# The expert stage of a two-layer trunk: norm weights ahead of the gather, token weights at the read-out, pairs summed in PSUM

## The chip, the cores and the metric

One core of a Trainium2 chip runs the whole program. The metric is the device time of one execution in microseconds; less is better. All weights are read from HBM once. The engines named below are TensorE (matmuls), VectorE, ScalarE, GpSimd and SyncE, whose queue issues the weight transfers.

## The reference, cut

A trunk of two layers runs over 256 positions of width 1024. Each layer mixes (`w_in`, three kinds of heads, `w_out`), then has a feed-forward part (dense in layer 0, eight experts in layer 1, of which each token takes its best two), then a gated embedding. The change touches only the expert part of layer 1:

```python
def _moe_swiglu(x, router_w, wg, wu, wd):      # x: RMSNorm(h) * ffn_norm_g
    logits = (xt @ router_w).astype(jnp.float32)
    top_val, top_idx = lax.top_k(logits, TOP_K)
    gates = jax.nn.softmax(top_val, axis=-1)
    combine = jnp.einsum('nk,nke->ne', gates, jax.nn.one_hot(top_idx, N_EXPERTS))
    for e in range(N_EXPERTS):
        out = out + combine[:, e:e + 1] * _swiglu(xt, wg[e], wu[e], wd[e])
```

`_swiglu` is `(silu(x @ wg) * (x @ wu)) @ wd` with a hidden width of 3584.

## The kernel before

Matrix products use float32 numbers split into a rounded high half and a low half (type F32R), which TensorE takes in a single pass: hi x hi, hi x lo and lo x hi are summed in PSUM (`mm3`). Weights come in tiles of 128 x 2048 (1 MB). ScalarE makes `hi`, VectorE makes `lo` (`Feed.high`, `Feed.low`); nine tiles of raw weights (five `rawp`, four `rawb`) are in flight, and SyncE's queue loads the next when VectorE has done with one (`Feed.pump`, line 326).

The order of instructions is planned when the program is built. The main stream emits the matmuls; side streams (generators) emit everything else. `best` picks the side step with the least estimated start, and of equal ones the one with the smaller `pen`; `slot` lets steps in between two products; each engine then works its list in order.

The expert stage (`moe`) begins with the router: `choose` makes logits and the best two of each token, `ranks` counts tokens for each expert, sorts the experts by count (`order`, which the transfers of expert weights need) and gives each token a rank within its expert. `busy` adds a filler matmul of 512 columns of float32 that nothing reads. `normed` writes the normed tokens, without the norm's weights, as halves `ah` (named rh) and `al` (rl).

The eight experts are taken in four pairs (`FE`, `MOE`). Those with the most tokens (three, one in each of the first three pairs) have 128 slots, the others 64 (`SLOTS`). For a pair, `gather` makes one-hot matrices `P` from the ranks and `part` multiplies `ah` and `al` with them (32 matmuls of 256 columns into pgx), then `splits` multiplies by the norm's weights and splits again: 16 ScalarE and 16 VectorE instructions write `gx`. `turned` transposes P for the way back (`PT`).

Each expert has seven hidden blocks of 512. `gate_up` makes the two products (pmg, pmu), `gate` and `up` apply silu and multiply (msl) and split the result into `mt`; an expert with 64 slots keeps its two halves in one tile and folds them by eight small matmuls (msg, pht). `down` multiplies `mt` with the third matrix into pmy. After the seventh block `read_out` copies pmy (as two halves for 128 slots, whole for 64), `scatter` multiplies with PT into psc, and VectorE adds psc, times the token's weight `cp`, to `h`: eight additions for each pair.

The rank-sorted slots hold only 128 or 64 tokens. If an expert has more, `overflow` computes the rest in a general way: it is written out for all eight experts and two blocks, and stands behind a branch on the largest excess (line 1378, at the first products of expert 2). With the inputs given it is skipped.

In line 101 a helper issues all compute instructions, so views by line name it for nearly all of them; the names of the tiles tell them apart.

Of the kernel before, what the change touches and what calls it, by code (L numbers as in the profile page):

```python
# [22 lines left out]
NE = 8  # L23
# [41 lines left out]
def tile_trunk(ctx, tc, x, par, con, abias, wif, rw, pt, w1, w2, wgu, wdn, wpg, wpp, wm, out):  # L65
# [197 lines left out]
    nc.gpsimd.memset(ones, 1.0)  # L263
    euler = cst.tile([128, 1], F32, name="euler")
# [785 lines left out]
    def moe(L, X, nxt):  # L1050
# [11 lines left out]
        al = big.tile([128, 2, D], F32R, name="rl", tag="xh")  # L1062

        def normed(t):

            for f in range(2):
                s = slice(512 * f, 512 * f + 512)
                yield when(act, (X, t, "r"))
                act.activation(ah[:, t, s], h[:, t, s], AF.Copy, scale=X.of(t))
                yield when(dve, *[("ranks", 1) if f else ("order",)] * t)  # L1070
                dve.scalar_tensor_tensor(al[:, t, s], h[:, t, s], X.of(t), ah[:, t, s].bitcast(F32),
                                         op0=ALU.mult, op1=ALU.subtract)
                set_ready(("normed", t, f))

        def choose(t):
# [7 lines left out]
            busy(t)  # L1083
# [27 lines left out]
        def busy(t):  # L1111

            p = bank([128, 512], "busy")
            c, cur[0] = cur[0], None
            pe.matmul(p, lhsT=ident, rhs=h[:, t, 0:512], start=True, stop=True)
            cur[0] = c
            rel(p)

        def ranks():

            pr = bank([128, 3, NE], "prk")
            for t in range(2):
# [6 lines left out]
                busy(t)  # L1129
# [45 lines left out]
        Xe, PT, HT, SL, Y, YS = {}, {}, {}, {}, {}, {}  # L1175

        def gather(j2):

            P = F["P"].tile([128, 2, 2, 128], F32R, name="P", tag="P", bufs=1)
            for t in range(2):  # L1180
                yield when(dve, ("ranks", t))
                for j in range(2):
                    e = 2 * j2 + j
                    dve.tensor_scalar(P[:, t, j], iota if SLOTS[e] == 128 else twice, rp[:, t, e:e + 1], None,
                                      op0=ALU.is_equal)
            for j in range(2):
                e = 2 * j2 + j
                Xe[e] = big.tile([128, KT, 2, SLOTS[e]], F32R, name="gx", tag=("al", "xl")[j])
# [3 lines left out]
        def part(j2, P, k2):  # L1192
            ks = (2 * k2, 2 * k2 + 1)
            yield when(pe, ("normed", 0, k2 // 2), ("normed", 1, k2 // 2))
            p = bank([128, 4, 128], "pgx")
            for i2, k in enumerate(ks):
                for t in range(2):
                    for i, a in enumerate((ah, al)):
                        pe.matmul(p[:, 2 * i2:2 * i2 + 2].rearrange("p a b -> p (a b)"),
                                  lhsT=a[:, t, 128 * k:128 * k + 128],  # L1200
                                  rhs=P[:, t].rearrange("p a b -> p (a b)"), start=t + i == 0, stop=t + i == 2)
            xs = [(Xe[2 * j2 + j][:, k], p[:, 2 * i2 + j, :SLOTS[2 * j2 + j]], g[:, k:k + 1])
                  for j in range(2) for i2, k in enumerate(ks)]
            yield from splits(*[(v[:, 0], v[:, 1], src, gk) for v, src, gk in xs])
            rel(p)
            set_ready(("X", j2, k2))

        def turned(e, P):
            yield when(pe, ("X", e // 2, KT // 2 - 1))
# [65 lines left out]
        def overflow():  # L1275

            def part(src):
                r = F["P"].tile([128, 512], F32, name="or", tag="myh")
# [3 lines left out]
            r2 = F["P"].tile([128, 2, NE], F32, name="r2", tag="r2", bufs=1)  # L1282
            dve.tensor_tensor(r2, rm, slots[:, None, :].to_broadcast([128, 2, NE]), op=ALU.subtract)
            for e, block in [(e, b) for b in range(2) for e in range(NE)]:
                if not e:
                    dve.tensor_scalar(r2, r2, -(64.0, 128.0)[block], None, op0=ALU.add)
                P = F["P"].tile([128, 2, 2, 128], F32R, name="oP", tag="P", bufs=1)[:, :, 0]
                p = bank([128, 2, 128], "opt")
                for t in range(2):
                    dve.tensor_scalar(P[:, t], iota, r2[:, t, e:e + 1], None, op0=ALU.is_equal)  # L1290
                    pe.transpose(p[:, t], P[:, t].bitcast(F32), ident)
                T = F["P"].tile([128, 2, 128], F32, name="oT", tag="myl")
                act.activation(T, p, AF.Copy)
                rel(p)
                xf = F["T"].tile([128, KT, 128], F32, name="oxf", tag="mt")
                y = F["T"].tile([128, 2, 512], F32, name="oy", tag="mt")
                dve.memset(y, 0.0)
                for k in range(KT):
                    s = slice(128 * k, 128 * k + 128)
                    p = bank([128, 128], "ogx")  # L1300
                    for t in range(2):
                        pe.matmul(p, lhsT=ah[:, t, s], rhs=P[:, t], start=t == 0, stop=False)
# [372 lines left out]
```

## Time and profile before

| | us |
|---|---|
| median of 3 runs | 1451.82 (1448.79 to 1453.56) |
| profiled execution | 1451.61 |
| its span in the profile | 1449.9 |
| TensorE busy in the span | 1378.6 (95%) |
| VectorE busy | 1217.4 (84%) |
| ScalarE busy | 1048.0 (72%) |

The trace lists every instruction with its start and duration and, in brackets, the idle time of its engine before it and what ended that. Matmuls are pipelined: their durations overlap, and the distance between two starts is the price of one. A float32 matmul is two records, a single-pass one is one record.

### The profile page before, as it was taken

Reading aid. Unit: us, or ns where it says so; the run is one execution under the profiler, and the core shown is the slowest. Engines: PE = TensorE matmul, PEld = TensorE weight load, DVE = VectorE, ACT = ScalarE, POOL = GpSimd, SP = SyncE. Lnnn points to the kernel's source line nnn. Section 1 sums busy time; section 2 is a strip of 40 time slices with the busy share of each in tenths; the row PEclk is TensorE's granted clock in tenths of the full one; section 3 lists DMA queues with packets and bytes.
Section 4 is the critical chain, followed back from the end, with each engine's and each line's share of the span. In section 5 each row is a group of like instructions: output and inputs, shape, how many; then the busy total and the mean of one; then the engine's idle time right before and its main releaser. Section 6 shows DMA issues by size and latency. Waiting matters only on the chain. (4 is left out here: it accounts for less than half of the span.)

```text
span 1449.9 us, 18234 instructions
## 1 busy us (share of the span) xinstructions
PE 1378.6 (95%) x6426; PEld 1114.1 (77%) x6426; DVE 1217.4 (84%) x1294; ACT 1048.0 (72%) x1221; POOL 57.0 (4%) x71
## 2 busy tenths in 40 slices
PE   7999999999998979999979999989999989999998
PEld 5777888888876758888858888877888877777666
DVE  5997645457899489999978999989999999999986
ACT  7766534346776478888857888877887887988874
POOL 0211000000032000000000000000000000000000
PEclk9999999999999899999989999999999999999999
DMA  9243555554440199999987999988999998999980
GB/s 357 88 145 124 203 178 200 177 200 146 158 156 4 57 422 421 421 421 421 421 316 285 421 421 415 410 334 338 401 420 419 411 400 304 419 421 421 421 336 29
DMA packets 62611, 437.18 MB, mean 302 GB/s; under 512 B 7088, under 2 KB 7984, under 8 KB 10672
## 3 DMA queue, kind: packets, MB, share of 16 engines
q1 hardware_dynamic: 62352, 435.42, 76.0%
q8 instruction: 52, 0.85, 0.2%
q0 software_dynamic: 160, 0.52, 0.1%
q14 instruction: 47, 0.39, 0.1%
HBM read 434.86 MB, written 1.05 MB: 301 GB/s over the span
## 5 line engine op out<-in xcount | busy, mean ns | idle before, releaser
L101 DVE TENSOR_TENSOR lo<-rawp,hi 128x2048 fp32r<-128x2048 f32 (+1 forms) x336 | 597.4, 1804 | 119.5 <-ACT hi L101 99.0
L101 ACT ACTIVATE hi<-rawp 128x2048 fp32r<-128x2048 f32 (+1 forms) x336 | 502.4, 1525 | 190.9 <-PE pg L101 34.9
L101 DVE TENSOR_TENSOR lo<-rawb,hi 128x2048 fp32r<-128x2048 f32 (+1 forms) x154 | 341.6, 2244 | 12.9 <-ACT hi L101 4.6
L101 ACT ACTIVATE hi<-rawb 128x2048 fp32r<-128x2048 f32 (+1 forms) x154 | 286.7, 1882 | 47.3 <-PE pmg L101 15.2
L101 PE MATMUL pmy<-hi,mt 128*128 128x512 f32 x616 | 229.9, 407 | 11.2 <-DVE mt L101 11.1
L101 PE MATMUL pmg<-hi,gx 128*128 128x512 f32 x616 | 221.7, 398 | 7.5 <-DVEq L1378 5.9
L101 PE MATMUL pmu<-hi,gx 128*128 128x512 f32 x616 | 220.1, 396 | 0.0
L101 PE MATMUL pmu<-lo,gx 128*128 128x512 f32 x448 | 177.2, 396 | 9.1 <-DVE lo L101 8.5
L101 PE MATMUL pmg<-lo,gx 128*128 128x512 f32 x448 | 177.8, 397 | 8.1 <-DVE lo L101 8.0
L101 PE MATMUL pmy<-lo,mt 128*128 128x512 f32 x448 | 180.3, 403 | 0.7 <-DVE lo L101 0.7
L101 PEld LDWEIGHTS pmy<-hi,mt 128*128 128x128 f32 x616 | 119.5, 194 | 36.8 <-DVE mt L101 12.3
L101 PEld LDWEIGHTS pmg<-hi,gx 128*128 128x128 f32 x616 | 116.4, 189 | 32.6 <-issue 7.4
L101 PEld LDWEIGHTS pmu<-hi,gx 128*128 128x128 f32 x616 | 115.8, 188 | 23.1 <-issue 0.5
L101 PEld LDWEIGHTS pmu<-lo,gx 128*128 128x128 f32 x448 | 84.2, 188 | 34.7 <-DVE lo L101 17.5
L101 PEld LDWEIGHTS pmg<-lo,gx 128*128 128x128 f32 x448 | 84.9, 190 | 32.6 <-DVE lo L101 15.5
L101 PEld LDWEIGHTS pmy<-lo,mt 128*128 128x128 f32 x448 | 87.2, 195 | 21.2 <-DVE lo L101 2.3
L101 PEld LDWEIGHTS pht<-conT,msg 128*128 128x128 f32 x560 | 73.2, 193 | 14.5 <-ACT msg L101 9.7
L101 PE MATMUL pht<-conT,msg 128*128 128x64 f32 x560 | 71.8, 272 | 5.7 <-ACT msg L101 5.6
L101 DVE SCALAR_TENSOR_TENSOR z<-zpad,parT,z 128x256 f32<-128x256 f32 x120 | 50.9, 477 | 0.3
L101 PE MATMUL pg<-hi,nh 128*128 128x512 f32 x96 | 37.7, 393 | 0.0
L101 PE MATMUL pg<-hi,nl 128*128 128x512 f32 x96 | 37.4, 390 | 0.0
L101 PE MATMUL pg<-lo,nh 128*128 128x512 f32 x96 | 37.4, 389 | 0.0
(299 smaller groups left out, 1882.1 us busy)
## 6 DMA issues: line engine op xcount, KB each, us to landing
rawp<-in_wm SPq DMA_DIRECT2D x184, 1024.0 KB, 8.8
rawb<-in_wm SPq DMA_DIRECT2D x148, 1024.0 KB, 9.0
rawp<-in_w SPq DMA_DIRECT2D x30, 1024.0 KB, 4.9
rawp<-in_wgu SPq DMA_DIRECT2D x22, 1024.0 KB, 4.9
rawp<-in_wdn SPq DMA_DIRECT2D x11, 1024.0 KB, 4.9
rawp<-in_wpg SPq DMA_DIRECT2D x5, 1024.0 KB, 4.8
rawp<-in_wm SPq DMA_DIRECT2D x8, 512.0 KB, 9.0
rawb<-in_wpg SPq DMA_DIRECT2D x3, 1024.0 KB, 12.1
```

The costliest lines, as they stand in the source:

```text
L101: return fn(*args, **kw)
```

## The change

- `normed` first multiplies h by the norm's weights (a copy in every partition, loaded by GpSimd's queue into `F["gain"]`), then makes the halves. The router's logits are made as before.
- `gather` keeps the halves apart: `part` multiplies `ah` and `al` with two windows of P, each of 192 columns (128 in the last pair), and one ScalarE copy for each of eight row blocks writes both halves of both experts. VectorE has no part in it.
- `weigh` multiplies the transposed one-hots with the token weights, so that `read_out` scales each slot while it copies pmy, in plain float32 for all experts.
- `scatter` sums both experts of each of the first three pairs in one PSUM tile (`together`), and VectorE adds that to h unscaled.
- `up` and `gate` of an expert's last block get pen -4 in place of -1.
- The splits of the first weight tile may start after half of the gather.
- `busy` issues a number of matmuls of 256 single-pass columns of ones: 12 and 10 in `choose`, 4 and 24 in `ranks`.
- The general way becomes one loop of 56 passes (expert and hidden block) over all tokens, and the count is loaded into registers after the first products of expert 1.

```diff
         def normed(t):
             for f in range(2):
                 s = slice(512 * f, 512 * f + 512)
+                yield when(dve, (X, t, "turned"))
+                dve.tensor_tensor(hg[:, t, s], h[:, t, s], F["gain"][f], op=ALU.mult)
                 yield when(act, (X, t, "r"))
-                act.activation(ah[:, t, s], h[:, t, s], AF.Copy, scale=X.of(t))
+                act.activation(ah[:, t, s], hg[:, t, s], AF.Copy, scale=X.of(t))
                 yield when(dve, *[("ranks", 1) if f else ("order",)] * t)
-                dve.scalar_tensor_tensor(al[:, t, s], h[:, t, s], X.of(t), ah[:, t, s].bitcast(F32),
+                dve.scalar_tensor_tensor(al[:, t, s], hg[:, t, s], X.of(t), ah[:, t, s].bitcast(F32),
                                          op0=ALU.mult, op1=ALU.subtract)
...
-        def busy(t):
+        def busy(n):
             p = bank([128, 512], "busy")
             c, cur[0] = cur[0], None
-            pe.matmul(p, lhsT=ident, rhs=h[:, t, 0:512], start=True, stop=True)
+            for _ in range(n):
+                pe.matmul(p[:, 0:256], lhsT=spare[:, 0:128], rhs=spare, start=True, stop=True)
...
-            side(*[part(j2, P, k2) for k2 in range(KT // 2)], pen=-3)
-            side(*[turned(2 * j2 + j, P[:, :, j]) for j in range(2)], pen=1)
+            side(*[part(j2, P, k) for k in range(KT)], pen=-3)
+            PE2 = [P[:, :, own[j]:own[j] + 128] for j in range(2)]
+            side(*[turned(2 * j2 + j, PE2[j]) for j in range(2)], pen=1)
+            side(weigh(j2, PE2), pen=1)
+
+        def part(j2, P, k):
+            yield when(pe, ("normed", 0, k // 4), ("normed", 1, k // 4))
+            n, win, _, _ = columns(j2)
+            p = bank([128, 2, n // 2], "pgx")
+            for i, a in enumerate((ah, al)):
+                for t in range(2):
+                    pe.matmul(p[:, i], lhsT=a[:, t, 128 * k:128 * k + 128], rhs=P[:, t, win[i]:win[i] + n // 2],
+                              start=t == 0, stop=t == 1)
+            yield act
+            x = XP[j2, k]
+            if n == 384:
+                act.activation(x, p.rearrange("p a b -> p (a b)"), AF.Copy)
+            else:
+                act.activation(x.rearrange("p (j a c) -> p a j c", j=2, a=2),
+                               p.rearrange("p a (j c) -> p a j c", j=2), AF.Copy)
+            rel(p)
+            set_ready(("X", j2, k))
+
+        def columns(j2):
+            m = [SLOTS[2 * j2 + j] == 128 for j in range(2)]
+            if not any(m):
+                return 256, (64, 64), (0, 128), [(0, 0, 128), (1, 128, 256)]
+            a, b = (0, 1) if m[0] else (1, 0)
+            return 384, (64, 0), (64, 192) if m[0] else (192, 64), [(b, 0, 64), (a, 64, 192), (b, 192, 320)]
+
+        def weigh(j2, P):
+            yield when(pe, ("comb", 0), ("comb", 1))
+            p = bank([128, 2, NE], "pws")
+            for j in range(2):
+                for t in range(2):
+                    pe.matmul(p[:, j], lhsT=P[j][:, t].bitcast(F32), rhs=cp[:, t], start=t == 0, stop=t == 1)
+            yield act
+            w = F["P"].tile([128, 2, NE], F32, name="ws", tag="ws")
+            act.activation(w, p, AF.Copy)
...
-                    side(fn(e, f, p), pen=-1)
+                    side(fn(e, f, p), pen=-4 if f == NF - 1 else -1)
+            if (e, f) == (1, 0):
+                emitted(("count",))
+                more.append(nc.values_load(cni[0:1, 0:1], min_val=0, max_val=S))
             if (e, f) == (2, 0):
                 emitted(("PT", 2), ("PT", 3), ("SC", 1, 0), ("SC", 1, 1))
                 cur[0] = None
-                with tc.If(nc.values_load(cni[0:1, 0:1], min_val=0, max_val=S) > 64):
+                with tc.If(more[0] > 64):
                     overflow()
...
         def read_out(e):
...
+            for n in range(2):
+                y = F["P"].tile([128, 512], F32, name="my", tag="my", bufs=4)
+                YS[e].append(y)
+                act.activation(y, Y[e][n], AF.Copy, scale=WS[e])
+                rel(Y[e][n])
...
+        def together(e):
+            return e < NE - 2 and SLOTS[e] != SLOTS[e ^ 1]
+
+        def scatter(es, t, N=None):
             for n in range(2):
...
+                for e in es:
+                    pe.matmul(p, lhsT=PT[e][:, t].bitcast(F32), rhs=YS[e][n], start=e == es[0], stop=e == es[-1])
                 yield dve
-                dve.scalar_tensor_tensor(h[:, t, s], p, cp[:, t, e:e + 1], h[:, t, s], op0=ALU.mult, op1=ALU.add)
+                dve.tensor_tensor(h[:, t, s], h[:, t, s], p, op=ALU.add)
...
         side(gather(0), pen=-3)
         emitted(("X", 0, 3))
-        feed.hold, feed.keep = len(seq), False
+        feed.hold, feed.keep = first_moe + 1, False
+        emitted(("X", 0, 7))
+        feed.hold = len(seq)
```

In the general way, for each pass of the loop, VectorE has two products with silu, four additions to h and two copies that move the weights on by one; ahead of the loop it has nine instructions. Before, it had 28 for each of 16 passes that were written out one after another.

## Rows read from the trace of the kernel before

**Rows 1.** The page, second part: GB/s moved in 40 slices of 36.2 us.
```profile
GB/s 357 88 145 124 203 178 200 177 200 146 158 156 4 57 422 421 421 421 421 421 316 285 421 421 415 410 334 338 401 420 419 411 400 304 419 421 421 421 336 29
```
**Rows 2.** Stretches of 10 us: busy PE, PEld, DVE, ACT, POOL; PEclk, DMA, GB/s.
```profile
680.00:690.00 10.00, 10.00 (x52) 8.32 (x51) 10.00 (x6) 9.65 (x10) 0.00 (x0) 1.00 1.01 419
...
730.00:740.00 10.00, 6.30 (x17) 5.01 (x18) 7.14 (x11) 5.06 (x7) 0.00 (x0) 0.66 0.73 300
...
760.00:770.00 10.00, 7.90 (x28) 6.41 (x29) 4.80 (x3) 4.75 (x4) 0.00 (x0) 0.69 0.17 57
...
880.00:890.00 10.00, 9.06 (x44) 7.22 (x43) 9.19 (x5) 7.58 (x6) 0.00 (x0) 1.00 1.02 422
...
960.00:970.00 10.00, 6.17 (x33) 5.04 (x33) 9.96 (x22) 8.12 (x19) 0.00 (x0) 0.88 0.91 338
...
1190.00:1200.00 10.00, 6.56 (x25) 5.05 (x24) 7.91 (x21) 6.82 (x12) 0.60 (x1) 0.83 0.88 337
```
**Rows 3.** Timeline of PE, changes of pair: start us, us, instruction, idle before.
```profile
733.70 0.79 PE L101 MATMUL pmy<-hi,mt 128*128 128x512 f32 x1 [3.83 <-DVE mt L101]
...
739.87 0.39 PE L101 MATMUL psc<-myh,PT 128*128 128x512 f32 x1
...
968.82 0.79 PE L101 MATMUL pmy<-hi,mt 128*128 128x512 f32 x1 [3.83 <-DVE mt L101]
...
1195.55 0.50 PE L101 MATMUL pmy<-hi,mt 128*128 128x512 f32 x1 [3.44 <-DVE mt L101]
```
**Rows 4.** The chain that ended last, in order of time: start us, us, matmuls.
```profile
762.10 5.80 PE pmg L101 x16
...
968.82 6.51 PE pmy L101 x16
...
995.64 3.66 PE pmu L101 x16
...
1195.55 5.53 PE pmy L101 x16
```
**Rows 5.** Timelines of DVE and of ACT at the first change of pair.
```profile
727.43 2.79 DVE L101 SCALAR_TENSOR_TENSOR gx<-pgx,parT,gx 128x128 fp32r<-128x128 f32 x12
...
733.23 0.41 DVE L101 TENSOR_TENSOR mt<-msl,mt 128x256 fp32r<-128x256 f32 x1
733.56 1.28 DVE L101 TENSOR_TENSOR myl<-pmy,myh 128x512 fp32r<-128x512 f32 x2
...
729.21 0.47 ACT L101 ACTIVATE mt<-msl 128x256 fp32r<-128x256 f32 x1
```
**Rows 6.** Instructions of line 1378 by engine (ns, start us), and PE's next matmul.
```profile
L1378 PEldq COMPARE_BRANCH  x1: 5512/5512/5512, 751.3 to 751.3; - x1
...
L1378 DVEq COMPARE_BRANCH  x1: 72/72/72, 756.9 to 756.9; - x1
...
L1378 DVEq EVENT_SEMAPHORE  x1: 21/21/21, 761.9 to 761.9; - x1
...
762.10 0.77 PE L101 MATMUL pmg<-hi,gx 128*128 128x512 f32 x1 [5.87 <-DVEq L1378]
```
**Rows 7.** Timeline of PE: small, gather and scatter matmuls.
```profile
491.20 1.85 PE L101 MATMUL prl<-rwT,nf 128*128 128x8 f32 x16
...
725.05 0.28 PE L101 MATMUL pgx<-P,rl 128*128 128x256 f32 x1
725.17 0.28 PE L101 MATMUL pgx<-P,rh 128*128 128x256 f32 x1
...
754.36 1.88 PE L101 MATMUL psc<-my,PT 128*128 128x512 f32 x4
```
**Rows 8.** Timelines of PE, DVE and ACT in the router and the first products.
```profile
494.83 1.95 PE L101 MATMUL busy<-h,conT 128*128 128x512 f32 x2
...
499.09 0.17 DVE L101 CAST order<-key 128x8 int32<-128x8 f32 x1
...
529.32 1.92 ACT L101 ACTIVATE hi<-rawp 128x2048 fp32r<-128x2048 f32 x1 [0.85 <-DMA rawp<-in_wm]
```

More of the change, by code (lines that the diff above doesn't have):

```diff
@@ L1173, in moe @@
         side(combine(0), combine(1), pen=-2)
[L1175 removed]
+        XP, PT, HT, SL, Y, YS, WS = {}, {}, {}, {}, {}, {}, {}
         def gather(j2):
[L1179 removed]
+            n, _, own, cs = columns(j2)
+            P = F["P"].tile([128, 2, 320], F32R, name="P", tag="P", bufs=1)
             for t in range(2):
                 yield when(dve, ("ranks", t))
[L1182 removed]
+                for j, c, d in cs:
@@ L1190, in gather @@
-            side(*[turned(2 * j2 + j, P[:, :, j]) for j in range(2)], pen=1)
[L1192 to L1196, printed above, removed]
-                for t in range(2):
[L1198 to L1204, printed above, removed]
+            for i in range(2):
+                x = big.tile([128, KT // 2, n], F32R, name="gx", tag=("al", "xl")[i])
+                for k in range(KT // 2):
+                    XP[j2, KT // 2 * i + k] = x[:, k]
@@ new lines, in overflow @@
+            with tc.For_i(0, NE * NF, 1) as i:
+                xf = []
+                for t in range(2):
+                    x = F["T"].tile([128, KT, 128], F32, name="oxf", tag="mt")
+                    xf.append(x)
+                    for k4 in range(2):
+                        p = bank([128, 4, 128], "ogx")
+                        for k in range(4):
+                            s = slice(512 * k4 + 128 * k, 512 * k4 + 128 * k + 128)
+                            pe.matmul(p[:, k], lhsT=ah[:, t, s].bitcast(F32), rhs=ident, start=True, stop=False)
+                            pe.matmul(p[:, k], lhsT=al[:, t, s].bitcast(F32), rhs=ident, start=False, stop=True)
+                        act.activation(x[:, 4 * k4:4 * k4 + 4], p, AF.Copy)
+                        rel(p)
+                pp = []
+                for u in range(2):
+                    pp.append([bank([128, 512], "ogu") for _ in range(2)])
+                    for k in range(KT):
+                        r = part(w[i, u, k // 4, :, 512 * (k % 4):512 * (k % 4) + 512])
+                        for t in range(2):
+                            pe.matmul(pp[u][t], lhsT=xf[t][:, k], rhs=r, start=k == 0, stop=k == KT - 1)
+                hT = []
+                for t in range(2):
@@ L1348, in product @@
                 if SLOTS[e] == 128:
-                    mm3(outs, x[:, 0], x[:, 1], [(hi[:, k, n], lo[:, k, n]) for n in range(len(outs))], first, last)
+                    mm3(outs, *x, [(hi[:, k, n], lo[:, k, n]) for n in range(len(outs))], first, last)
                 else:
@@ L1367, in gate_up @@
                     n = hl[0].shape[1] // 512
-                    for k2 in range(k // 2, (k + n) // 2):
-                        wait(("X", e // 2, k2))
-                    product(e, [p], [halves(e, Xe[e][:, i]) for i in range(k, k + n)], hl, k == 0, k + n == KT)
+                    for i in range(k, k + n):
+                        wait(("X", e // 2, i))
+                    product(e, [p], [tokens(e, i) for i in range(k, k + n)], hl, k == 0, k + n == KT)
                     k += n
@@ L1454, in moe @@
                 if f == NF - 1:
-                    side(read_out(e), *[scatter(e, t, N) for t in range(2)], pen=-4 if N else 0)
+                    es = [e]
+                    if together(e):
+                        es = [e - 1, e] if e % 2 else []
+                    side(read_out(e), *[scatter(es, t, N) for t in range(2 if es else 0)], pen=-4 if N else 0)
         emitted(("Y", NE - 1))
```

135 lines of the change are left out of this document (51 added, 84 removed).

## The prediction
> **What bounds the kernel now.** First the page's slices of bandwidth, for dips: from the fifteenth slice on (the expert stage) the transfers run at about 421 GB/s, with dips at 316 and 285, at 334 and 338, and at 304 [rows 1]. Then the table by stretches of 10 us: in the steady part (680 to 690) TensorE is busy 10.00 of 10.00 at clock 1.00 and the transfers go at 419 GB/s, so weights and matmuls are level; in stretches of the dips TensorE is busy only 6.2 to 7.9, its clock is as low as 0.66, and VectorE is the busier of the two in three of the four [rows 2]. These dips are the changes from one pair of experts to the next. What is to be won lies there and at the start; in the steady part the change alters nothing.
>
> Next, TensorE's order of instructions at the three changes of pair: the first down product of the last hidden block waits 3.83, 3.83 and 3.44 us for the VectorE step "mt" [rows 3]. The reader should see why: VectorE does 12 instructions gx (2.79 us), a weight split and four more gx before the "mt" of 0.41 us at 733.23; ScalarE put its own half of mt at 729.21 [rows 5]. [...] Last, the branch around the general way, which runs once, at the first change: VectorE's sequencer branches at 756.9, its next event is at 761.9, and TensorE stands idle 5.87 us for it [rows 6]; the sixteen matmuls that follow take 5.80 us, again the lower level [rows 4].
>
> **The change part by part.**
>
> *The norm weights ahead of the gather, and "last silu first".* The gathered columns come out of the matmul already weighted and already as high and low halves, so VectorE's 16 gx instructions for each pair go, and ScalarE's 16 become 8 wider ones (off the path: ScalarE waits for TensorE in these stretches). The up step of the last block gets the highest priority, so ScalarE's mt can follow VectorE's msl, which needs only the fold. VectorE then has at most one weight split ahead of mt (about 2 us; ScalarE's share of one takes 1.92 [rows 8]): it ends by about 727, and TensorE needs it at 729.9 (733.70 - 3.83). All three waits go, and with them the slow clock. Price: 3.83 + (6.17 - 3.66) = 6.3; 3.83 + (6.51 - 3.66) = 6.7; 3.44 + (5.53 - 3.66) = 5.3; together -18.3 us. Late next are the weight splits, which ScalarE makes while it now waits for TensorE, and the gathered columns, eight ScalarE copies that the next gate product needs.
>
> *The branch.* The count is loaded into registers earlier, and the general way shrinks from sixteen unrolled passes over expert and block to one loop: VectorE's part from 16 x 28 = 448 operations to 17 (2 + 7 ahead of the loop, 8 in it). If the gap from 756.9 to 761.9 is the price of jumping over that much code, it shrinks from 5.0 us to nearly nothing; TensorE's own branch record (5.5 us, from 751.3) already lies beside its queued matmuls and leaves about 1 us of the 5.87 [rows 6]. Bounds: 0 to 5 us gone; I take 4.9, since the skipped code is what shrinks, and with it 5.80 - 3.66 = 2.1 us of slow clock: -7.0 us.
> [...]
>
> *The scatter.* The three experts with 128 slots (one in each of the first three pairs) now read out in plain float32. Per pair and output tile this was one float32 matmul and two single-pass ones, and becomes two float32 ones. Two float32 matmuls (four records) take 1.88 us, 0.94 each; a single-pass one is 3.66 / 16 = 0.23 [rows 4, 7]. Four tiles: 8 x 0.94 - (4 x 0.94 + 8 x 0.23) = +1.9 us of TensorE. Token weights for the read-out: four tiny float32 matmuls, eight records at 1.85 / 16 = 0.116 [rows 7]: +0.9. Summing a pair in PSUM saves VectorE four of eight additions to h, and the low halves of the read-out (two) go: six instructions of 512 columns at 1.28 / 2 = 0.64, and 16 gx at 2.79 / 12 = 0.23 [rows 5], 7.5 us at each change. That pays only where VectorE is the bound, at the third (busy 7.9, TensorE 6.6 [rows 2]), where the last pair begins: I take -1.5, between 0 and -3.
>
> *The narrower gather.* Still 32 matmuls, of 192 columns (128 in the last pair) where 256 stood. At full clock they start 0.12 us apart [rows 7]. No row has a single-pass matmul under 256 columns. From below: 0.12 x 192 / 256 = 0.09. From above: the float32 rate, 0.94 x 192 / 512 = 0.35. I take 0.116, the spacing at which even eight-column matmuls with fresh weights go [rows 7]: a change of nothing. So TensorE's extra work is 1.9 + 0.9 = 2.8 us in each of the first three pairs, +8.4 us, all on the path because TensorE is the bound there. In the last pair it idles beside VectorE: nothing.
>
> *The router.* The filler matmuls ahead of the ranks shrink: two fillers, the second of 1.95 us at slow clock [rows 8], become 10 + 4 matmuls of 256 columns, 14 x 0.12 = 1.7 us or twice that, so the expert order (499.09 [rows 8]) comes 0.4 to 2 us earlier, and the first weights with it: they are fetched by that order. The gather, in turn, gets a longer filler of 24 (2.9 to 5.8 us, beside VectorE's ranks) and one late chain: the second half's product with the norm weights, its ScalarE copy and its difference now follow the order one after another (three steps of about 0.64 us; TensorE gathers the first half meanwhile). Four more VectorE products of 512 columns (0.64 each [rows 5]) fit into its idle time before the logits; if not, +2.6. The split of the first weights no longer waits for all of the gather and for 16 gx, so the first product starts some 3 us earlier. But ScalarE waits for transfers as late as 529.32 [rows 8], so the stage is fed by the transfers until then, and only their earlier start counts: I take -2, bounds 0 and -5.
>
> *Nothing:* loading the norm weights (two transfers on GpSimd's queue while no weights move), the start-up copy for the fillers, the earlier register load (0.5 us on sequencers that run ahead). If the norm weights landed late, the router would wait for them: they are half a megabyte, and a whole one takes 2.5 us at 421 GB/s [rows 1], so +2.5 at most.
>
> **The sum.** -18.3 - 7.0 + 8.4 - 1.5 - 2.0 = -20.4 us on the profiled execution of 1451.6 us (span 1449.9 plus 1.7): 1431 us. It lies 0.2 us from the median of the runs shown (1451.8), so the same number stands for both.
>
> **The rivals.**
> [...]
> 2. *Something else is late instead of mt.* Eight gathers need eight PSUM banks in turn, each freed by a ScalarE copy among splits of 1.92 us; before, four parts did. If the down or gate product waits half as long and still falls to the slow clock, half of 18.3 comes back: 1440. Against it: ScalarE has idle time right after the changes.
> 3. *The narrow gather runs at the float32 rate* (the other side). Place: TensorE's in-order queue at all four gathers. Price: (0.35 - 0.12) x 32 = 7.4 us at the second and third; 128 columns at 0.235: 3.7 at the last; the first 32 x 0.35 = 11.2 against 6.8 now, +4.4, and the 2 us of the router are gone: +24.9 us, so 1456; at slow clock in the first gather 11 more, 1467. It decides from 0.28 us per gather matmul on (20.4 / 128 above 0.12). For it: every single-pass matmul of the trace has 256 columns or more. Against it: the single-pass kind is one record per matmul at every width that is there, the float32 kind two.
> The plan also shifts, since priorities change the order everywhere: near 885 TensorE loses 0.9 us of ten to late splits [rows 2], and so in the last blocks of the second and third pair, some three in each; that could vanish (-6) or appear elsewhere (+6).
>
> **How the numbers follow.** Chances: the forecast 0.57, rival 1 0.14, rival 2 0.14, rival 3 0.10, something not foreseen 0.05. About 0.3% (4.4 us) is what a measurement can tell from no change. Faster by more than that: the forecast, rival 1 and nearly all of rival 2, 0.82; within it: the low half of rival 3 and the tail of rival 2, 0.08; slower: the rest, 0.10. The range runs from 1419 (the router's 5, VectorE's 3 and the plan's 6 all won) to 1456 (the gather's upper bound).
>
> **What would show it.** Right: no wait of pmy for mt at the three changes, clock 1.00 in those stretches, a gap after VectorE's branch well under 1 us, gather matmuls about 0.12 us apart, some 7 us of scatter per pair. Wrong: a gather matmul over 0.28 us, a gap of 4 to 5 us left after the branch, a new wait of a similar size in front of the first gate product of a pair, or steady stretches in which TensorE is less busy than the 10.00 of now.

## The result, and the profile after

| | before | after |
|---|---|---|
| median, us | 1452.69 (1448.79 to 1456.11, 4 runs) | 1434.07 (1433.16 to 1434.86, 4 runs) |
| span of the profiled execution, us | 1449.9 | 1432.2 |

The ratio is 0.9872, with a 95% interval of 0.9846 to 0.9899: 18.6 us faster, where 20.4 were forecast (1431, range 1419 to 1456).

The page's slices of bandwidth, to be held against [rows 1], and stretches of 10 us, against [rows 2] (columns as there):
```profile
GB/s 361 89 147 126 206 176 195 187 183 170 145 147 30 16 402 421 420 422 420 421 417 337 420 407 417 406 388 319 413 415 408 402 402 367 418 420 422 421 310 30
```
```profile
730.00:740.00 10.00, 10.00 (x51) 8.40 (x50) 8.09 (x4) 10.00 (x12) 0.00 (x0) 1.00 1.02 423
...
960.00:970.00 10.00, 10.00 (x45) 7.76 (x45) 6.88 (x3) 9.47 (x12) 0.00 (x0) 1.00 1.01 428
...
1190.00:1200.00 10.00, 10.00 (x40) 6.42 (x40) 7.26 (x7) 5.95 (x8) 0.00 (x0) 1.00 0.93 350
```
In each pair of dips one slice is filled or nearly so (417, 388), the single dip is shallower (367), and TensorE is busy 10.00 of 10.00 at clock 1.00 where it was busy 6.2 to 6.6 at 0.66 to 0.88. From 700 to 1400 us these are the largest waits of TensorE that are left (for whom: us in total, times, longest):
```profile
PE pmg L101 <- DVE lo L101: 9.8, 19, 0.7
PE pmu L101 <- DVE lo L101: 8.3, 10, 0.9
PE pmg L101 <- DVEq L1420: 0.9, 1, 0.9
```
No wait of the second product for "mt" is left [rows 3]; what is left are low weight splits that come a little late. The branch (line 1420 now) by engine, and TensorE's next matmul in its timeline, against [rows 6]:
```profile
L1420 PEldq COMPARE_BRANCH  x1: 455/455/455, 742.8 to 742.8; - x1
...
L1420 DVEq COMPARE_BRANCH  x1: 72/72/72, 750.3 to 750.3; - x1
L1420 DVEq EVENT_SEMAPHORE  x1: 21/21/21, 751.0 to 751.0; - x1
```
```profile
751.15 0.47 PE L101 MATMUL pmg<-hi,gx 128*128 128x512 f32 x1 [0.93 <-DVEq L1420]
```
Gather matmuls of 192 columns (first change) and of 128 (third), the token weights and the scatter of a pair, against [rows 7]:
```profile
721.12 0.39 PE L101 MATMUL pgx<-P,rl 128*128 128x192 f32 x2
721.34 0.39 PE L101 MATMUL pgx<-P,rh 128*128 128x192 f32 x2
...
1171.14 0.39 PE L101 MATMUL pgx<-P,rl 128*128 128x128 f32 x2
1171.36 0.38 PE L101 MATMUL pgx<-P,rh 128*128 128x128 f32 x2
...
730.88 0.95 PE L101 MATMUL pws<-cp,P 128*128 128x8 f32 x8
...
743.19 7.03 PE L101 MATMUL psc<-my,PT 128*128 128x512 f32 x16
```
Two gather matmuls take 0.22 us at either width, 0.11 each.

Where the 17.7 us of span went, by starts of the same instruction in the two traces: +1.4 up to the last sum of the mixing (486.71, now 488.11), -3.0 from there to the first change of pair, -11.3, -4.2 and -4.6 at the three changes (to the next pair's first pmy), +1.3, +1.8 and +1.5 in the pairs between and behind them, -0.6 at the end.

### The profile page after: what moved, and what is told of

Read it like the earlier page. It is cut to its first block, busy times and chain, and to the rows that moved or that the text cites. A ratio compares the mean times of both kernels' runs of the same rounds, so it can differ in the third digit from the quotient of the medians.

```text
span 1432.2 us, 18251 instructions
## 1 busy us (share of the span) xinstructions
PE 1379.7 (96%) x6500; PEld 1118.2 (78%) x6500; DVE 1197.2 (84%) x1222; ACT 1045.5 (73%) x1194; POOL 58.2 (4%) x73
## 5 line engine op out<-in xcount | busy, mean ns | idle before, releaser
L101 PE MATMUL pmy<-hi,mt 128*128 128x512 f32 x616 | 224.1, 398 | 0.1
L101 PE MATMUL pmy<-lo,mt 128*128 128x512 f32 x448 | 175.6, 392 | 0.5 <-DVE lo L101 0.3
L101 PEld LDWEIGHTS pmy<-hi,mt 128*128 128x128 f32 x616 | 115.8, 188 | 23.7 <-DVE mt L101 0.7
L101 PEld LDWEIGHTS pmy<-lo,mt 128*128 128x128 f32 x448 | 84.2, 188 | 19.7 <-DVE lo L101 1.8
```

What stands on the lines that cost most here:

```text
L101: return fn(*args, **kw)
```

## The experiments

All times in one table. "To order" is the time in the profiled execution from the last sum of the mixing (VectorE's second h<-h,pwo) to the expert order, "to end" that from the same sum to the end of the span. That sum starts anywhere from 484.0 to 490.5 us in the fourteen profiles, where the programs up to it are nearly the same; these two columns leave that out. Each ratio is to the kernel before as it was run beside that kernel; its medians there lie between 1451.3 and 1453.6 us.

| kernel | median, us (range) | ratio to before | to order | to end |
|---|---|---|---|---|
| before | 1452.7 | | 12.38 | 963.2 |
| after | 1434.1 (1433.2 to 1434.9) | 0.9872 [0.9846, 0.9899] | 11.20 | 944.1 |
| e1_unrolled | 1439.9 (1439.2 to 1444.5) | 0.9921 [0.9900, 0.9942] | 11.20 | 949.5 |
| e2_late_number | 1436.4 (1433.2 to 1439.0) | 0.9890 [0.9866, 0.9913] | 11.21 | 944.2 |
| e3_silu_not_first | 1437.7 (1434.2 to 1439.0) | 0.9897 [0.9870, 0.9923] | 11.20 | 947.2 |
| e4_before_silu_first | 1437.5 (1433.6 to 1440.9) | 0.9893 [0.9863, 0.9922] | 14.03 | 949.5 |
| e5_two_small_parts | 1441.3 (1439.0 to 1444.3) | 0.9928 [0.9902, 0.9954] | 14.30 | 951.7 |
| e6_scatter_two_passes | 1433.9 (1433.3 to 1435.3) | 0.9882 [0.9850, 0.9914] | 11.21 | 943.1 |
| e7_first_parts_up_front | 1436.6 (1436.3 to 1437.2) | 0.9898 [0.9874, 0.9922] | 11.20 | 946.6 |
| e8_transfer_estimate | 1424.7 (1418.5 to 1425.8) | 0.9801 [0.9766, 0.9836] | 11.20 | 934.6 |
| e9_fillers_and_shift | 1432.2 (1429.2 to 1438.4) | 0.9864 [0.9837, 0.9891] | 11.20 | 944.7 |
| e10_estimate_lower_still | 1426.8 (1425.2 to 1431.3) | 0.9820 [0.9790, 0.9850] | 15.91 | 942.9 |
| e11_estimate_and_two_passes | 1429.0 (1426.2 to 1431.7) | 0.9839 [0.9807, 0.9870] | 15.95 | 943.3 |
| e12_shift_and_estimate | 1424.2 (1422.6 to 1425.8) | 0.9800 [0.9780, 0.9821] | 11.21 | 935.4 |

**The jump undone (e1).** On the kernel after:
```diff
-            with tc.For_i(0, NE * NF, 1) as i:
+            for i in range(NE * NF):
```


> The changed kernel, with one thing undone: the general way is written out 16 times again and no longer a loop, so that the jump over it is long again; the number for the branch is still fetched into the registers a block earlier. Theory (the length of the jump costs the time): TensorE's gap at the branch is near 5 us again instead of 0.7, VectorE and TensorE resume some 4 us later, and some 2 us of slow-clock work behind the gap come back: 1438 to 1441 us, so 4 to 7 above the changed kernel's 1434. Rival (the early fetch of the number took the gap away, the jump itself is free): the gap stays under 1 us and the time at 1434, give or take 2.

The edit writes out the loop's 56 passes and not, as the text above says, the 16 longer ones of the kernel before: VectorE passes over 627 instructions here, over 773 in the kernel before and over 48 in the one after (counted in the built programs).

1439.9 us, 5.8 more than after, and 5.4 more to the end. The branch by engine (ns, start us), and TensorE's next matmul:
```profile
L1420 PEldq COMPARE_BRANCH  x1: 6219/6219/6219, 744.2 to 744.2; - x1
...
L1420 DVEq COMPARE_BRANCH  x1: 72/72/72, 751.7 to 751.7; - x1
L1420 DVEq EVENT_SEMAPHORE  x1: 21/21/21, 756.1 to 756.1; - x1
```
```profile
756.24 0.77 PE L101 MATMUL pmg<-hi,gx 128*128 128x512 f32 x1 [4.60 <-DVEq L1420]
```
The gap on VectorE is 4.4 us again, with the number fetched early, and the first matmul behind it takes 0.77 us instead of 0.47, as behind the gap of the kernel before (0.77, where the granted clock was 0.65 from 762.1 to 767.9 us). The branch stands at the same place in the programs of TensorE and VectorE as in the kernel after, so the jump over the written-out way is what costs; the rival falls.

**The early number undone (e2).** The fetch into registers goes back to the branch:
```diff
-            if (e, f) == (1, 0):
-                emitted(("count",))
-                more.append(nc.values_load(cni[0:1, 0:1], min_val=0, max_val=S))
...
-                with tc.If(more[0] > 64):
+                with tc.If(nc.values_load(cni[0:1, 0:1], min_val=0, max_val=S) > 64):
```


> The changed kernel, with one thing undone: the number for the branch is fetched into the registers right ahead of the branch again; the general way stays a loop. Theory (the prediction priced the fetch at the 2.1 us that stood ahead of the branch before and the jump at 4.9): a gap of 2 to 3 us at the branch, with a little slow clock behind it: 1436 to 1437 us. Rival (a late fetch is as dear as the whole gap was): 1439 to 1441. Rival (the fetch runs ahead of the work, since TensorE and VectorE get there at other times now): 1434.

The text above has one thing wrong: the 2.1 us of the prediction were slow clock, and the fetch stood under "nothing" there. 1436.4 us, though the profiled execution has the same 944.2 to the end as after (944.1); TensorE's gap is 1.41 us in place of 0.93 and not the 2 to 3 of the theory, and VectorE's fetch takes 0.54. So the early number is worth half a microsecond in the trace; the medians (2.3 us apart) say no more than that it is not much.

**"Last silu first" undone (e3), and alone (e4).** On the kernel after, and on the one before:
```diff
-                    side(fn(e, f, p), pen=-4 if f == NF - 1 else -1)
+                    side(fn(e, f, p), pen=-1)
```
```diff
-                    side(fn(e, f, p), pen=-1)
+                    side(fn(e, f, p), pen=-4 if f == NF - 1 else -1)
```


> The changed kernel, with one thing undone: the chains behind the last block's two sums (silu, product, turned hidden values) get the same weight in the order of the work as those of the other blocks, -1 and not -4. Theory (both parts were needed: the chain goes ahead of the next pair's gather, and VectorE has less work of the gather): the second-product matmuls wait again for the hidden tile at the three changes of pair, 1 to 4 us at each with some slow clock behind it: 1438 to 1446 us. Rival (ScalarE's copy for both halves of the gather, without VectorE's part, took the wait away by itself): the waits stay under 0.5 us and the time at 1434, give or take 2.

> The kernel before, with one part of the change alone: the chains behind the last block's two sums get the weight -4 in the order of the work and not -1; the gather, the read-out and the general way are as before. Theory (the order alone takes most of the wait): the waits for the hidden tile of 3.8, 3.8 and 3.4 us at the three changes go, with the slow clock behind them, 12 to 18 us: 1434 to 1440 us. Rival (VectorE then has the gathered tokens' subtractions still to do, and TensorE waits for the tokens in place of the hidden tile): new waits of TensorE for gathered tokens of 2 to 4 us at each change, and 1447 to 1453 us.

TensorE's waits from 700 to 1400 us, first of e3, then of e4:
```profile
PE pmg L101 <- DVEq L1420: 2.4, 1, 2.4
PE pmy L101 <- DVE mt L101: 0.6, 2, 0.3
```
```profile
PE pmg L101 <- DVEq L1378: 5.1, 1, 5.1
PE pht L101 <- ACT msg L101: 1.5, 3, 0.7
PE psc L101 <- DVE h L101: 1.4, 1, 1.4
...
PE pmy L101 <- DVE mt L101: 0.6, 1, 0.6
```
Either part removes the waits for "mt" nearly whole: 11.1 us of them before, 0.6 with the order alone (e4), 0.6 with the rest of the change and without the order (e3). The theory of e3, that both are needed, falls. The rival's waits under 0.5 us are there, but not its 1434 us: of the 3.1 us more to the end, 2.5 arise at the branch (a wait of 2.4 us in place of 0.9, and a granted clock of 0.83 in place of 1.00 from 750 to 760 us). The last line of ScalarE's timeline ahead of the branch's events, and the events (ns, start us), in e3:
```profile
751.86 1.91 ACT L101 ACTIVATE hi<-rawp 128x2048 fp32r<-128x2048 f32 x1 [4.26 <-PE pmu L101]
```
```profile
L1420 DVEq COMPARE_BRANCH  x1: 72/72/72, 751.7 to 751.7; - x1
...
L1420 ACTq EVENT_SEMAPHORE  x1: 17/17/17, 753.8 to 753.8; - x1
L1420 DVEq EVENT_SEMAPHORE  x1: 21/21/21, 754.0 to 754.0; - x1
```
The undone order has put a weight split of 1.91 us late on ScalarE; ScalarE's event follows that split, and VectorE's event follows ScalarE's by 0.2 us. That the one waits for the other fits these times; no run tests it. In e4 nothing of that size comes in place of "mt": its rival, that gathered tokens would be waited for, falls too. One number changed in the kernel before gave some 14 of the 18.6 us.

**The two small parts together (e5), and the same with another place for the jump (e9).** e5 is the kernel before with the weight -4, the loop and the early number. e9 adds the change's fillers in the router and, ahead of the first transpose, nine matmuls of 8 columns:
```diff
+    for _ in range(9):
+        nc.tensor.matmul(pad[:, 0:8], lhsT=ones, rhs=ones[:, 0:8], start=True, stop=True)
...
-            busy(t)
+            busy((12, 10)[t])
...
-                busy(t)
+                busy((4, 24)[t])
```


> The kernel before with two parts of the change: the chains behind the last block's sums get the weight -4, and the general way is the loop, with the number for the branch fetched a block earlier (tokens scaled by the norm weight there, since the gather is still as before). The gather, the tokens' splits, the read-out and the scatter stay as before. Theory (the order and the jump are the whole gain; what the rest takes from VectorE and adds to TensorE comes to nothing): the run with the order alone, 1437.5, less the 4 to 6 us that the written-out way cost: 1431.5 to 1434 us, the changed kernel's time. Rival (the new gather and read-out bring some 3 to 6 us by themselves that the order alone does not): 1436 to 1440. Rival (the scatter's extra TensorE time is a net loss): 1426 to 1430.

> The kernel before with the two small parts of the earlier run (last silu first; the loop with the early number), now also with the change's short fillers in the router, and with nine tiny matmuls on TensorE ahead of the first transpose, where it waits for the input. Fillers and tiny matmuls put the branch at instruction 6917 of TensorE's program in place of 6798 (the changed kernel has it at 6910; it passes over 342 and 344 instructions). The gather, the splits of its tokens, the read-out and the scatter stay as before. In the earlier run TensorE's own jump still took 5.9 us. Theory (where the short jump lies in TensorE's program decides whether it is dear; the fillers hold the clock in the router): TensorE's branch record under 0.6 us and its gap 1 to 2.5 us in place of 4.8; the expert order 11.2 us after the last sum of the mixing, in place of 14.3; 1441.3 less 3 for the router, less 3 to 6 for the jump: 1432 to 1436 us. Rival (TensorE's jump is dear because the engine comes to it late, with nothing queued, wherever it lies): the record stays near 5 us and the time at 1437 to 1439. Rival (the new gather and scatter are a net loss of some 3 us): 1428 to 1431.

e5 was a miss on the far side, 1441.3 us. Its trace says why: the branch of TensorE, its next matmul, and the expert order in VectorE's timeline, first of e5, then of e9:
```profile
L1380 PEldq COMPARE_BRANCH  x1: 5882/5882/5882, 755.8 to 755.8; - x1
```
```profile
762.01 0.77 PE L101 MATMUL pmg<-hi,gx 128*128 128x512 f32 x1 [4.81 <-PEq L1380]
```
```profile
503.69 0.17 DVE L101 CAST order<-key 128x8 int32<-128x8 f32 x1
```
```profile
L1386 PEldq COMPARE_BRANCH  x1: 454/454/454, 753.9 to 753.9; - x1
```
```profile
756.73 0.47 PE L101 MATMUL pmg<-hi,gx 128*128 128x512 f32 x1 [1.39 <-DVEq L1386]
```
```profile
499.84 0.17 DVE L101 CAST order<-key 128x8 int32<-128x8 f32 x1
```
The places 6798, 6917 and 6910 in the text above, and its 342 and 344 instructions, are those of the loop inside the skipped code. In the built programs the branch itself stands 14 instructions ahead of them, at 6784 in e5, 6903 in e9 and 6896 in the kernel after, and passes over 367, 367 and 370. The 119 between e5 and e9 stay.

In both the jump has the same length, and in both TensorE reaches it late, with the last matmuls of its scatter just issued. In e5 it took 5.9 us, in e9, 119 instructions further on in the program, 0.45. So neither the length alone nor what is queued decides; the place in the program is what differs near the branch. The fillers and tiny matmuls that moved it are the only other difference, some 250 us and more earlier, and e5 is the only kernel with the short jump at the dear place. The ten kernels here that have the loop and TensorE's branch at 6896 to 6903 (after, e2, e3, e6 to e12) have 0.36 to 0.46 us. Which places are dear, no run here shows.

From e5 to e9 the time to the end falls by 7.0 us. The order comes 3.1 us earlier, but only 1.1 us of that are left at the last block of the first pair (its first gate matmul starts 225.2 and 224.1 us after the sum of the mixing); behind the jump e9 is 7.2 us ahead. So some 6 us belong to the jump: 3.4 to the gap (4.81 and 1.39), the rest to the lower clock behind it: from the first gate matmul there to the first up matmul e5 takes 6.84 us and e9 4.21, and e5's granted clock is 0.66 from 760 to 770 us.

e9's 1432.2 us and 944.7 to the end are the changed kernel's 1434.1 and 944.1, with the gather, the splits of the tokens, the read-out and the scatter of before; the first weight splits, too, wait for the whole gather again. So in the total those five edits come to nothing here; the gain is the order, the jump and the router. Place by place they do not. The first gate matmul in the last block of each pair, in us after the sum of the mixing (e8 and e12 are the same two kernels with another number in the planner, below):

| pair | after | e9 | e9 later by | e8 | e12 | e12 later by |
|---|---|---|---|---|---|---|
| first | 219.8 | 224.1 | 4.3 | 219.6 | 221.3 | 1.7 |
| second | 444.8 | 447.3 | 2.5 | 442.7 | 441.6 | -1.0 |
| third | 669.7 | 670.6 | 0.9 | 661.6 | 658.9 | -2.7 |
| last | 882.7 | 882.6 | -0.1 | 870.2 | 869.9 | -0.3 |

The five edits gain 4.3 and 1.7 us up to the end of the first pair (after and e1, the same program up to there, differ by 0.8), and cost 1.7 to 2.8 us from each of the first two pairs to the next. Which of the five does which, no run separates.

**The scatter in two passes (e6).** On the kernel after, each expert by itself:
```diff
-                act.activation(y, Y[e][n], AF.Copy, scale=WS[e])
+                act.activation(yh, Y[e][n], AF.Copy, scale=WS[e])
+                yield dve
+                dve.scalar_tensor_tensor(yl, Y[e][n], WS[e], yh.bitcast(F32), op0=ALU.mult, op1=ALU.subtract)
...
-            return e < NE - 2 and SLOTS[e] != SLOTS[e ^ 1]
+            return False
```


> The changed kernel with the read-out the other way: each expert's weighted result is split into two float32r parts (ScalarE the first, VectorE the difference), scattered with two single passes of some 0.23 us each, expert by expert, in place of one float32 product of 0.88 us and a sum of a pair in PSUM. TensorE's scatter work per pair falls from 7.0 us to some 3.7; VectorE gets some 5.5 us more per pair (four differences and four more sums of 0.69 us). Theory (the prediction's: TensorE's time counts one for one where nothing waits): three pairs times 3.3 us less, and as much again once for the last pair: 1422 to 1426 us. Rival (VectorE's 5.5 us come back as later weight splits at the change of pair): 1431 to 1437. Rival (the order by which ScalarE and VectorE work shifts for the worse): 1438 to 1445.

1433.9 us, 1.0 less to the end: the time of the first rival, though not by later weight splits. TensorE had 3.3 us less to do per pair and waited instead:
```profile
PE pmg L101 <- DVE lo L101: 9.5, 19, 0.6
PE pmu L101 <- DVE lo L101: 8.2, 11, 0.9
PE psc L101 <- DVE myl L101: 4.5, 2, 2.8
```
The waits for low splits stayed as they were (17.7 us, 18.1 in the kernel after), and 4.5 us for the new low halves came in addition. TensorE's time, taken off at the price of work for VectorE, does not count one for one in these pairs.

**The first gather's halves up front (e7).** On the kernel after, one loop in two:
```diff
                 act.activation(ah[:, t, s], hg[:, t, s], AF.Copy, scale=X.of(t))
+            for f in range(2):
+                s = slice(512 * f, 512 * f + 512)
                 yield when(dve, *[("ranks", 1) if f else ("order",)] * t)
```


> The changed kernel with the order of one helper turned: the product with the norm weight and the first split of the tokens are made for both halves of a token tile up front, so that only the last difference of the second half waits for the counts. In the changed kernel TensorE waited 2.9 us and then 0.8 us for these in the first gather, and its first expert product started 3.2 us later than before instead of earlier. Theory (TensorE is the bound from the first product on): the first product some 3 us earlier, and the time 1431 to 1432. Rival (until the first pair's fourth block it is the transfers that set the pace, at 2.5 us a tile): the first product earlier, the second-product matmuls of the first expert where they were, and 1434 give or take 1.5.

The first product starts 6.6 us earlier (506.41, after 512.97, at nearly the same order), the first second-product matmul 1.7 us later (541.57, after 539.88), and the time is 2.5 us longer. The early work waits in portions, and the clock goes down behind it (TensorE's timeline, and a stretch of 10 us, which has 1.00 in the kernel after):
```profile
532.74 1.29 PE L101 MATMUL pht<-conT,msg 128*128 128x64 f32 x8 [2.70 <-ACT msg L101]
```
```profile
530.00:540.00 10.00, 5.86 (x29) 4.96 (x28) 7.01 (x13) 7.45 (x8) 0.00 (x0) 0.83 1.02 422
```
Starting early where the transfers set the pace (424, 421 and 422 GB/s in the stretches from 510 to 540 us) gained nothing and cost a little: worse than the rival.

**The planner's transfer time (e8, e10, e11, e12).** One number; e10 has 2.35, e11 is e6 with 2.5, e12 is e9 with 2.5:
```diff
-                self.dma = max(self.dma, self.free[which].pop(0)) + 2.65
+                self.dma = max(self.dma, self.free[which].pop(0)) + 2.5
```


> The changed kernel with one number of its planner changed: a weight tile is taken to arrive every 2.5 us and not every 2.65 us (the trace moved 421 GB/s, 2.49 us a tile of 1 MB). Only the order of instructions changes. Theory (the waits of 0.3 to 0.9 us of TensorE for the low weight split, some 18 us in the expert stage, come from splits put too late in ScalarE's and VectorE's order): 3 to 8 us fewer: 1426 to 1431 us. Rival (these waits follow the real arrival of the weights, whatever the order): 1434 give or take 2. Rival (splits put ahead of the tokens' chains delay those instead): 1436 to 1442.

1424.7 us, 9.4 under the changed kernel, more than the theory's 3 to 8. TensorE's waits from 700 to 1400 us in e8:
```profile
PE pht L101 <- ACT msg L101: 5.7, 9, 1.7
PE pmu L101 <- DVE lo L101: 2.7, 9, 0.4
...
PE pmg L101 <- DVE lo L101: 0.3, 1, 0.3
```
18.1 us of waits for low splits became 3.0, and 5.7 for msg came. How the late ones arise is seen near 934 us in the kernel after, first in ScalarE's timeline, then in the chain that ended last; the third fence is ScalarE's timeline in e8 at the same block:
```profile
933.18 0.60 ACT L101 ACTIVATE mt<-pht 128x512 fp32r<-128x512 f32 x1 [2.15 <-PE pht L101]
```
```profile
933.68 1.92 ACT hi L101
...
935.62 2.30 DVE lo L101
...
937.97 1.89 PE pmu L101 x7
```
```profile
930.51 5.51 ACT L101 ACTIVATE hi<-rawp 128x2048 fp32r<-128x2048 f32 x3
```
ScalarE stands 2.15 us at "mt" with a high split queued behind it; the low split then follows, and TensorE last, 0.94 us late. With the right arrival the plan puts three high splits into that time.

> The changed kernel with the planner's number for a weight tile at 2.35 us; at 2.65 the time was 1434, at 2.5 it was 1424.7, and the trace has 2.49. Theory (what counts is that the planned arrival is right): 2.35 is as far off as 2.65 on the other side, splits are then put ahead of what they have to wait for: 1427 to 1436 us. Rival (the earlier the weights' splits stand in the order the better): 1419 to 1424. Rival (it was one lucky order): anything from 1425 to 1442.

> The changed kernel with both: the planner's 2.5 us for a weight tile, and the read-out in two float32r parts scattered with single passes (which alone left the time at 1433.9, its span 0.7 us under the changed kernel's). Theory (with the splits in time TensorE is the bound in the pairs, and its 3.3 us less per pair now count): 1424.7 less 4 to 9: 1416 to 1421 us. Rival (what VectorE has to do in addition takes it back, as it did alone): 1423 to 1427. Rival (the order comes out worse): 1428 to 1436.

> The kernel before with the three small parts (last silu first; the loop with the early number, its jump placed by the tiny matmuls; the short fillers), as in the run that gave 1432.2, and with the planner's 2.5 us for a weight tile, which took the changed kernel from 1434.1 to 1424.7. Gather, splits of the tokens, read-out and scatter are those of before. Theory (the new gather, read-out and scatter come to nothing, whatever the planner's number): 1421 to 1427 us. Rival (with the weights' splits in time VectorE is what is short, and its 7.5 us per change of pair, which the change takes from it, now count): 1428 to 1436 us. Rival (with the splits in time TensorE is what is short, and the extra scatter of some 2 us per pair counts): 1415 to 1420 us.

e10 (1426.8) came out between its theory and its first rival, and e11 (1429.0) at its last rival: its theory, that TensorE's 3.3 us per pair count once the splits are in time, falls. In the profiled executions of both the router took 4.7 us longer than in e8 (below), and even with these taken off they have some 3.6 and 3.9 us more to the end than e8. Their ratios' intervals overlap with e8's. So it is not shown that 2.35 is worse than 2.5, nor that it would be so because the arrival is wrong. In all four kernels with a number under 2.65 the median is lower than in the same kernel with 2.65, by 4.9 to 9.4 us; that speaks against one lucky order. e12 is at e8's time (1424.2), within its theory: with the planner's number at 2.5, too, the old gather and scatter are as good in the total as the new ones. e8 and e12 are faster than both kernels.

## Why the prediction was right, point by point

**The waits for "mt" (-18.3).** They went, with the lower clock behind them. In the kernel before the sixteen matmuls behind each wait took 739.87 - 733.70 = 6.17 us [rows 3], 6.51 and 5.53 [rows 4], at a granted clock of 0.58, 0.57 and 0.69, against 3.66 at 1.00 (995.64 to 999.30 us); these are the matmul times in its price. The mechanism was right, the size some 4 us too large: e4, which removes little else, has 13.7 us less to the end than before, or 14.3 from the end of the first pair on, where it is 0.6 us behind (its order comes 1.65 us later). The prediction gave the credit to two edits together; either alone does it.

**The branch (-7.0).** Undone it cost 5.4 to 5.8. The price of the gap was right (5.87 us became 0.93, 4.9 were forecast), and the reading that the jump, not the fetch of the number, makes it. That the gap shrinks with the skipped code was an estimate; e1 bears it out (on VectorE 4.4 us over 627 instructions, 0.7 over 48). But it took TensorE's own jump as hidden beside queued matmuls; e5 shows that it can stand on the path for most of its length (4.8 of 5.9 us) behind the short loop; with the branch 112 instructions earlier in TensorE's program, where e5 has it, some 6 of the 7.0 us might have stayed (an estimate from e5 and e9); the chance of 0.14 for rival 1 was for all of them, 1438.

**The changes of pair.** Forecast from those terms and 2.8 us of scatter each: -10.5, -3.9, -4.0; measured -11.3, -4.2, -4.6.

**The scatter (+8.4) and VectorE's relief (-1.5).** The durations were right (7.03 us for a pair's scatter, 0.95 for the weights), the step that failed is "all on the path because TensorE is the bound there", and with it "only at the third" for VectorE. The prediction's own rows have VectorE busier than TensorE at all three changes (7.14 and 6.30, 9.96 and 6.17, 7.91 and 6.56 [rows 2]). e6 takes 3.3 us per pair off TensorE and gets 1.0 us in all, with 4.5 us of new waits for VectorE; e9 and e12 leave the old gather and scatter and are level with after and e8 in the total. By the table of e9 the new edits together cost 1.7 to 2.8 us from each of the first two pairs to the next, where 2.8 us of TensorE's time were forecast, and gain about as much elsewhere. Whether the scatter cost nothing, or cost what was forecast and VectorE's relief paid for it, the runs do not separate. The sum came out since this term and that of "mt" were both too large, with opposite signs: that it lies within 1.8 us of the measured gain is in part luck.

**"In the steady part the change alters nothing."** It gave back 4.6 us there. In the kernel before, TensorE's waits for low splits from 700 to 1400 us are
```profile
PE pmg L101 <- DVE lo L101: 7.3, 15, 0.6
PE pmu L101 <- DVE lo L101: 6.4, 9, 0.9
```
which is 13.7 us, against 18.1 after: 4.4 more, nearly all that was given back. So the order in the pairs came out worse, within the plus or minus 6 that the prediction had set for the plan; e8 shows what a better one is worth.

**The narrow gather (0).** Right: 0.11 us at 192 and at 128 columns. Rival 3 had its threshold at 0.28.

**The router (-2).** The order comes 1.2 us earlier after the mixing, within the 0.4 to 2 forecast, and the blocks of the first pair 3.0 us. e9, whose order comes as early and whose gather and first splits are the old ones, is 4.3 us later there than after, so the order did not bring that gain. "The first product starts some 3 us earlier" was wrong: measured from that sum it starts 1.8 us later. In ScalarE's list the first weight splits stand ahead of the second half's rh, and TensorE's gather waits for it (timelines of ScalarE and of TensorE, after):
```profile
505.92 1.99 ACT L101 ACTIVATE hi<-rawp 128x1024 fp32r<-128x1024 f32 x2
507.81 0.71 ACT L101 ACTIVATE rh<-hg,nr 128x512 fp32r<-128x512 f32 x1
```
```profile
508.58 0.53 PE L101 MATMUL pgx<-P,rh 128*128 128x192 f32 x1 [2.86 <-ACT rh L101]
```
That it cost nothing, because the transfers feed the stage until some 530 us, was the prediction's next step, and e7 bears it out; in the kernel after, ScalarE still waits for a transfer at 527.75 and 530.07 us (0.31 and 0.41), and the transfers go at 426 and 419 GB/s from 510 to 530. The prediction put slow work at twice the time; in the kernel before, behind the waits for "mt" it was 1.5 to 1.8 times (5.53 to 6.51 us against 3.66), and in e10's router, at a granted clock of 0.57, the sixteen matmuls of the logits took 3.42 us against 1.84 in the kernel after.

**The range.** Its lower end is a slip: 1431.2 less 3, 1.5 and 6 is 1420.7; 1419 comes out when the same is taken off the span.

**Ahead of the stage** the prediction had nothing; the 1.4 us there lie inside the 6.5 us by which that point varies from profile to profile.

## What to carry to other kernels

When a wait vanishes after a change with several edits, try each edit alone: here one number in the planner's weights was worth most of the rewrite, and another, the arrival time of a transfer, half as much again. A table in which TensorE reads 10.00 of 10.00 in most stretches may still hold many short waits (in the kernel after every third stretch from 840 to 940 us reads 9.06); work taken off it bought little here where VectorE got work for it (e6: 3.3 us less per pair, 1.0 us in all). The jump over skipped code had a price on each engine by itself, 0.36 to 6.2 us in TensorE's branch record and 0.5 to 5.0 from VectorE's branch to its next event: read every engine's branch record, also after edits elsewhere that only shift the program.

## What the runs showed that was not expected

**A jump's place.** 367 skipped instructions of TensorE cost 5.9 us at one place and 0.45 us 119 instructions further on. On VectorE, with 47 or 48 skipped, the next event came 0.5 to 1.5 us behind the jump in eight kernels and 2.3 us in three (e3, e8, e10); in these three it comes 0.2 us behind ScalarE's event, as shown for e3. Why the eight differ is open.

**The router's clock.** With the old fillers the order came 12.38, 14.03 and 14.30 us after the mixing in three profiles; with the new ones it came at 11.20 or 11.21 in nine, and at 15.91 and 15.95 in two. In these two the same fillers run at the lower level, as TensorE's timeline of e10 has it:
```profile
490.18 2.51 PE L101 MATMUL busy<-spare 128*128 128x256 f32 x12
492.49 3.42 PE L101 MATMUL prl<-rwT,nf 128*128 128x8 f32 x16
```
and in the kernel after at the full one:
```profile
491.65 1.67 PE L101 MATMUL busy<-spare 128*128 128x256 f32 x12
493.15 1.84 PE L101 MATMUL prl<-rwT,nf 128*128 128x8 f32 x16
```
The stretch 490 to 495 has a granted clock of 0.57 in e10 and 1.00 in after, with TensorE busy 5.00 of 5.00 in both and the same kinds of work ahead of it. What decides is not shown.
